# Small sums in two groups, the dt products ahead of turn 4, and the last norm's weights rest on VectorE, in a hybrid decoder layer

## The chip, the cores and the metric

The kernel runs on one core of a Trainium2 chip, in float32. A core has TensorE (PE in the profile, its weight loads PEld), VectorE (DVE), ScalarE (ACT) and GpSimd (POOL); all DMAs here are issued from SyncE's queue (SP). The metric is the device time of one execution in microseconds, the median of three runs. The time before is 1727.1 us (1726.97 to 1727.77).

## What is computed

One decoder layer over 16 learned tokens and 1024 input tokens, D = 1024:

```python
xn = rms_norm(h, mix_pre_g)
proj = xn @ w_in                       # z, xbc, dt, q, k, v
y_ssd = ssd_mixer(z, xbc, dt_raw, ...)           # conv, scan in chunks of 128, rms_norm
y_sb = rms_norm(stick_breaking_attention(q, k, v), sb_norm_g)
mix = concatenate([y_ssd, y_sb]) @ w_out
h = h + rms_norm(mix, mix_post_g)
xn = rms_norm(h, ffn_pre_g)
gu = xn @ w_up
g = causal_dwconv(gu[..., :D_FF], ffn_conv_w, ffn_conv_b)
f = (gelu(g) * gu[..., D_FF:]) @ w_down
h = h + rms_norm(f, ffn_post_g)
return h[:, N_META:]
```

with `rms_norm(x, g) = x * rsqrt(mean(x * x) + EPS) * g`. The two norms inside the mixer (of y_ssd and of y_sb) are not applied to the activations: their gains are multiplied into the rows of `w_out`, and their scales per token, r_ssd and r_sb, are applied to the product.

## The kernel before

Products run on TensorE with both operands cut in two: a high part, rounded on ScalarE, and a **rest**, value minus high part, made by a subtraction on VectorE or GpSimd. A product is then high x high, high x rest of x, rest of w x high. Weights come in blocks of 128 columns; a raw block, its high part and its rest each live in a ring of buffers (`wraw` 2, `whi` 3, `wlo` 3).

**The opening** (lines 231 to 339) has an order written out by hand on all engines: each engine runs its instructions in the order of the source. `norms[i]`, i = 0 to 8, is one block of tokens (block 0 the learned ones). For each: `square` (ScalarE, with a sum along the row), `root` (GpSimd: add EPS, then a power), `norm` (VectorE: times the scale and the gain), `turn_x` (TensorE: eight transposes of 128x128 into two PSUM tiles; ScalarE copies the high halves into `xs`, VectorE subtracts the rests). The products of dt over the first 400 columns (`dt_steps`: 16 products, `pj_dt`) need blocks 0 to 3 in full, high parts and rests, and a weight whose two halves (`wh_dt`) are the high part and the rest. B and C are two column blocks of the next projection; `split_hi` and `split_lo` cut their weights, the rest in two halves on GpSimd. In iteration i of the loop, norm i + 2, turn i and square i + 3 come in this order, with exceptions for i = 3.

**The small sums.** `token_rstd` makes r_ssd and r_sb: `sq` holds squares summed over the blocks of 128 channels, and nine products with a column of ones sum them over the partitions, one column of a PSUM tile each (the program splits each float32 product into two passes). Two VectorE instructions and a power on GpSimd follow. It is called once in the attention (head pair 0, block 2; only TensorE's order is by hand there) and once while the first half of W_out is multiplied, when n is 2 in the loop over `first`, whose steps are 12 products each. `issue_after` puts its products behind the last one issued. Its PSUM tile comes from the ring `mm` that the projections use.

**The last norm of the second sub-layer's input** (lines 1457 to 1600) stands in the last part that is ordered by hand on all engines. `after(t, ...)` is a generator with five steps: square and root of the mixed rows; scale and residual on VectorE; a second square; its root; the second norm. `turn_x2(t, ...)` transposes the result. For t = 8 its steps are run between the first products of the next matrix: `g0_first` (a product into a bank, an evacuation by ScalarE, a second product added into the same bank, an evacuation). `g0` and `u0` are the first blocks of the gate and up weights; `split_1` and `split_2` cut them, high parts on ScalarE and rests on GpSimd. The order of the weights of W_out is not touched.

Of the kernel before, what the change touches and what calls it, by code (L numbers as in the profile page):

```python
# [53 lines left out]
def tile_layer(ctx: ExitStack, tc: tile.TileContext, x, meta, rows, parts,  # L54
# [162 lines left out]
    def dt_steps(hl):  # L217
        for c0, n in CH:
            acc = psum_mm(f"pj_dt_{c0}")
            for k in range(KB):  # L220
                for j in range(2):
                    mm(acc[:32, :n], hl[:, k, :], xs[c0][:, j, k, :n],
                       start=(k == 0 and j == 0), stop=(k == KB - 1 and j == 1))
            nc.vector.tensor_copy(dtT[:, c0:c0 + n], acc[:32, :n])
            yield

    ET = mybir.EngineType
    with tc.tile_pool(name="pre", bufs=3, side="right") as pre, \
# [82 lines left out]
        norm(0)  # L311
        norm(1)
        for i in range(NT + 1):
            if i != 3:
                norm(i + 2)
            turn_x(i)
            square(i + 3)
            root(i + 3)
            if i == 3:
                norm(5)  # L320
            if i == 1:
                hl = wp.tile([P, KB, 32], F32R, tag="whi", name="wh_dt", bufs=WB)
                nc.scalar.activation(hl[:, :, 0:16], raw_dt, AF.Copy)
                nc.gpsimd.tensor_tensor(hl[:, :, 16:32], raw_dt, hl[:, :, 0:16].bitcast(F32), op=ALU.subtract)
                dt_chain = dt_steps(hl)
            if i in (2, 5):
                split_hi("B0" if i == 2 else "C0")
            if i in (2, 3, 5, 6):
                split_lo("B0" if i < 4 else "C0", int(i in (3, 6)))
            if i == 3:  # L330
                chains.append(conv_chain(8, "B0", ws["B0"], True))
            if i == 4:
                run(dt_chain, 1)
            if i in (5, 6):
                run(chains[0][1], 1)
            if i == 6:
                chains.append(conv_chain(10, "C0", ws["C0"], True))
            if i in (7, 8):
                run(chains[1][1], 1)
# [98 lines left out]
        post = []  # L438
        return qkv_steps(p, post), post

    def token_rstd(r, pool, nm):
        pt = psum_mm(f"pt{nm}")
        for t in range(NT + 1):
            a, nr = (M0, 2) if t == 0 else (NM + (t - 1) * P, P)
            mm(pt[:nr, t:t + 1], sq[:, a:a + nr], ones[:, 0:1], start=True, stop=True)
        ms = pool.tile([P, NT + 1], F32, tag="tms", name=f"tms{nm}")
        nc.vector.memset(ms[:, 0:1], 1.0)
        nc.vector.tensor_scalar(ms[:2, 0:1], pt[:2, 0:1], 1.0 / D, EPS, op0=ALU.mult, op1=ALU.add)
        nc.vector.tensor_scalar(ms[:, 1:], pt[:, 1:NT + 1], 1.0 / D, EPS, op0=ALU.mult, op1=ALU.add)
        nc.gpsimd.tensor_tensor(r, ms, nhalf[:, :NT + 1], op=ALU.pow)  # L450
# [553 lines left out]
    for p in range(8):  # L1004
        for i in range(NT):
# [52 lines left out]
            if p == 7 and 2 < i < 6:  # L1058
                run(meta_steps, 1)
            if p == 0 and i == 2:  # L1060
                token_rstd(r_ssd, ap, "a")
    while turn or mix:
        if mix:
            block_mix(*mix.pop(0))
# [33 lines left out]
    ys = [split_y(op, 1, 1, ("yh", "yl", 2))]  # L1098
    y0g = y0s[0]
    nc.vector.tensor_tensor(y0g, y0b, sb_g.unsqueeze(2).to_broadcast([P, 8, 2]), op=ALU.mult)  # L1100
    acc = psum_fa("halo1")[:, 0, 0:256]
    summed = []

    def halo_raw():
# [5 lines left out]
    for n, i in enumerate(first):  # L1110
# [1 line left out]
        if i == 1:  # L1112
            run(second, 2)
        with tc.issue_after(recent[0].ins):
            if n == 2:
                token_rstd(r_sb, est, "b")
            while n > 5 and len(summed) < rows_in:
                halo_raw()
    run(second)
# [346 lines left out]
    for t in range(1, NT + 1):  # L1466
# [44 lines left out]
        elif t == NT:  # L1511
            g0_pair = pair_w("2g0")
            u0.split_1()
            g0.split_2(g0_pair)
            load_raw(1, 1, wp, "wraw", 2)
        run(steps)
        if t == 6:
# [46 lines left out]
        return g0.first_half(ws, psum_fa(f"g0{ws[0]}"), ghalf[jj], part_g)  # L1564

    ga_ = g0_first(0, ("a11", "a12"))
    run(ga_, 1)
    run(norm, 2)
    split_b22(nc.vector)
    turn7 = turn_x2(7, P, xn7, x2_tiles(7))  # L1570
    run(turn7, 1)
# [339 lines left out]
```

## Time and profile before

| | before |
|---|---|
| median of 3 runs | 1727.1 us |
| profiled execution | 1726.21 us, span 1724.3 us |
| TensorE's granted clock, mean | 0.998 |
| VectorE, ScalarE, GpSimd busy | 65%, 48%, 49% |
| HBM read, written | 122.32 MB, 49.73 MB |

The span is the time from the first to the last instruction that was profiled; the profiled execution has its own time, and some 1.9 us lie around its span. In the views, a row has start, length, engine, line, operation, out<-in, and, in brackets, how long the engine stood idle before it and what ended that. Rows of equal instructions are merged (x8). Lengths of neighbours overlap by some hundredths to tenths, since an engine starts an instruction while the one before it drains; the ends of matmuls are modelled. L12 is line 12 of the kernel. `xtp` are the transposes of x, `xn` its norms, `xs` the turned x, `pj_` products of a projection, `x2tp` and `oxn` the transposes and norms of the second sub-layer's input.

### The profile page before, as it was taken

The numbers are of one execution on the slowest core, as the hardware profiler recorded it, in microseconds if no ns is written. First come the engines' busy times: TensorE is split into PE (matmuls) and PEld (weight loads), VectorE is DVE, ScalarE is ACT, GpSimd is POOL, SyncE is SP. The second block draws the span as 40 slices with busy tenths as digits, with TensorE's granted clock in tenths as the row PEclk, the third lists the DMA queues.
The fourth block names the chain that finished last, engine by engine and source line by source line (L and its number), as shares of the span: only waits on it lengthen the run. The fifth ranks groups of instructions, "written<-read, shape, count | busy, mean of one in ns | idle before, by whom it ended". The sixth has DMA issues, their size and how long they took to land. (4 is left out here: it accounts for less than half of the span.)

```text
span 1724.3 us, 28047 instructions
## 1 busy us (share of the span) xinstructions
PE 1703.0 (99%) x11230; PEld 1496.2 (87%) x11230; DVE 1117.8 (65%) x1233; ACT 821.2 (48%) x1370; POOL 850.4 (49%) x642
## 2 busy tenths in 40 slices
PE   7999999999999999999999999999999999999998
PEld 6999889888999998998788788999888888887886
DVE  5752973875676677578530567676666666658777
ACT  5423663555566566557652344433333333344544
POOL 4323664585566575565552122587767777400001
PEclk9999999999999999999999999999999999999999
DMA  4233343231011101112214653233332223395334
GB/s 164 58 111 98 105 127 108 68 105 38 26 38 38 36 28 38 38 50 86 64 68 147 212 174 123 73 107 110 103 92 92 92 92 99 118 330 180 105 113 179
DMA packets 90674, 173.87 MB, mean 101 GB/s; under 512 B 10704, under 2 KB 35816, under 8 KB 90544
## 3 DMA queue, kind: packets, MB, share of 16 engines
q1 hardware_dynamic: 90544, 172.08, 31.4%
q8 instruction: 88, 1.44, 0.4%
q14 instruction: 42, 0.34, 0.1%
HBM read 122.32 MB, written 49.73 MB: 100 GB/s over the span
## 5 line engine op out<-in xcount | busy, mean ns | idle before, releaser
L782 POOL TENSOR_TENSOR bt<-bt,kp 128x256 f32<-128x256 f32 (+7 forms) x128 | 213.0, 1683 | 185.7 <-DVE kp L780 144.3
L780 DVE TENSOR_TENSOR_SCAN kp<-kp,hold 128x272 f32<-128x272 f32 (+7 forms) x128 | 183.5, 1474 | 24.7 <-ACT kp L773 14.3
L1265 POOL TENSOR_TENSOR wlo<-wr,whi 128x1024 fp32r<-128x1024 f32 x43 | 107.7, 2516 | 37.8 <-ACT whi L1264 37.8
L1768 POOL TENSOR_TENSOR fms<-fms 128x1 f32<-128x1 f32 x8 | 2.6, 331 | 223.8 <-ACT dh L1653 197.1
L773 ACT ACTIVATE kp<-z 128x288 f32<-128x288 f32 (+6 forms) x112 | 82.6, 737 | 50.5 <-PE z L772 27.8
L1264 ACT ACTIVATE whi<-wr 128x1024 fp32r<-128x1024 f32 x43 | 45.6, 1060 | 111.5 <-PE fX L1322 67.9
L165 PE MATMUL pj_k<-xs,wh_k 128*128 128x400 f32 (+2 forms) x384 | 95.6, 336 | 0.0
L165 PE MATMUL pj_v<-xs,wh_v 128*128 128x400 f32 (+2 forms) x384 | 95.0, 334 | 0.0
L1394 DVE SCALAR_TENSOR_TENSOR ga<-gr,pp,ga 128x1024 f32<-128x1024 f32 x44 | 71.8, 1632 | 35.1 <-ACT ga L1387 34.3
L165 PE MATMUL pj_q<-xs,wh_q 128*128 128x386 f32 (+2 forms) x384 | 93.8, 331 | 0.0
L796 ACT ACTIVATE th<-tw 128x1024 f32<-128x1024 f32 (+2 forms) x96 | 75.6, 815 | 37.4 <-PE tw L794 37.3
L1653 ACT ACTIVATE dh<-ar 128x512 fp32r<-128x512 f32 x77 | 48.6, 631 | 92.9 <-PE dnB L1731 44.7
L165 PE MATMUL pj_X<-xs,wh_X 128*128 128x400 f32 (+2 forms) x384 | 92.0, 326 | 0.0
L165 PE MATMUL pj_z<-xs,wh_z 128*128 128x386 f32 (+2 forms) x384 | 91.6, 326 | 0.0
L748 DVE CAST qh<-q 128x128 fp32r<-128x128 f32 x64 | 45.5, 712 | 69.9 <-PE z L772 69.6
L1654 DVE TENSOR_TENSOR dl<-ar,dh 128x512 fp32r<-128x512 f32 x77 | 53.2, 691 | 50.2 <-ACT dh L1653 50.2
L966 PE MATMUL mo<-woa,yh 128*128 128x512 f32 x256 | 85.2, 400 | 0.0
L774 ACT ACTIVATE bt<-z 128x288 f32<-128x288 f32 (+6 forms) x112 | 82.9, 740 | 0.0
L794 PE MATMUL tw<-ident,bt 128*128 128x128 f32 x576 | 75.9, 274 | 2.2 <-POOL bt L782 1.6
L809 PE MATMUL av<-th,v 128*64 128x128 f32 x1152 | 77.2, 278 | 0.0
L809 PEld LDWEIGHTS av<-th,v 128*64 128x64 f32 x1152 | 61.5, 136 | 13.8 <-issue 10.9
L794 PEld LDWEIGHTS tw<-ident,bt 128*128 128x128 f32 x576 | 65.5, 141 | 8.6 <-issue 4.0
(560 smaller groups left out, 5623.9 us busy)
## 6 DMA issues: line engine op xcount, KB each, us to landing
wr<-in_w_up SPq DMA_DIRECT2D x44, 512.0 KB
fds<-ga SPq DMA_DIRECT2D x44, 256.0 KB
b<-in_w_down SPq DMA_DIRECT2D x44, 256.0 KB
ar<-fds SPq DMA_DIRECT2D x44, 256.0 KB
fda<-ga SPq DMA_DIRECT2D x33, 256.0 KB
ar<-fda SPq DMA_DIRECT2D x33, 256.0 KB
yk<-yd SPq DMA_DIRECT2D x16, 512.0 KB
wor<-in_w_out SPq DMA_DIRECT2D x12, 512.0 KB
```

The costliest lines, as they stand in the source:

```text
L165: mm(acc[:ncol, :n - s], a[:, k, :ncol], xs[c0][:, b, k, s:n], start=(k == 0 and j == 0), stop=(k == KB - 1 and j == 2))
L773: nc.scalar.activation(kp[:, :, a:a + w], z[:, :, :w], AF.Sigmoid, scale=-QSCALE)
L774: nc.scalar.activation(bt[:, :, a:a + w], z[:, :, :w], AF.Sigmoid, scale=QSCALE)
L780: nc.vector.tensor_tensor_scan(kp[:, j][:, ::-1], kp[:, j][:, ::-1], hold[:, L - n:L][:, ::-1], 0.0, op0=ALU.mult, op1=ALU.max)
L782: nc.gpsimd.tensor_tensor(bt[:, j, 0:m], bt[:, j, 0:m], kp[:, j, 1:m + 1], op=ALU.mult)
L794: nc.tensor.transpose(tw[:, j, b, :], bt[:, j, c0:c0 + P], ident)
L796: nc.scalar.activation(th[:, :, :nb, :], tw[:, :, :nb, :], AF.Copy)
L809: mm(av[halves[j], :], v[:, kb, halves[j]], th[:, j, b, :], start=kb == 0, stop=kb == i)
L966: recent[0] = mm(acc, u[:, k, :], v[:, cs], start=(k == 0 and j == 0), stop=(k == 7 and j == 2))
L1265: nc.gpsimd.tensor_tensor(l, raw, h.bitcast(F32), op=ALU.subtract)
L1394: nc.vector.scalar_tensor_tensor(v, self.g[jj][:, :, i:i + 256], fconv_w[:, j, i:i + 1], v, op0=ALU.mult, op1=ALU.add)
L1654: sub(lo[:, k], raw, hi[:, k].bitcast(F32), op=ALU.subtract)
```

## The change

- Opening: norm 4, square 5 and root 5 move from iterations 2 and 3 to the end of iteration 3, behind turn 3. The cut of B's weights moves from iterations 2 and 3 into iteration 3, with square 6 and root 6 between the two halves of its rest; that of C's from 5 and 6 to 4 and 5. The first 16 dt products go ahead of norm 6 and turn 4 on each engine's order, and take all the high parts of x first, then all the rests.
- `token_rstd` becomes a generator that stops after five of the nine products, and gets its PSUM tile from outside: a tile of the ring `tp` for r_ssd, the unused half of the tile `halo1` for r_sb. It is run in blocks 2 and 3 of head pair 0, and at n = 2 and n = 4.
- The rest of the second raw block of g0 (`g0_pair[1]`, wlo2g) is made by VectorE, in place of GpSimd.
- The first step of the last norm (square and root of t = 8) goes ahead of the first product of g0 and of its evacuation.

```diff
--- before.py
+++ after.py
@@ -217,10 +217,9 @@
     def dt_steps(hl):
         for c0, n in CH:
             acc = psum_mm(f"pj_dt_{c0}")
-            for k in range(KB):
-                for j in range(2):
-                    mm(acc[:32, :n], hl[:, k, :], xs[c0][:, j, k, :n],
-                       start=(k == 0 and j == 0), stop=(k == KB - 1 and j == 1))
+            for i in range(2 * KB):
+                j, k = (i // KB, i % KB) if c0 == 0 else (i % 2, i // 2)
+                mm(acc[:32, :n], hl[:, k, :], xs[c0][:, j, k, :n], start=i == 0, stop=i == 2 * KB - 1)
             nc.vector.tensor_copy(dtT[:, c0:c0 + n], acc[:32, :n])
             yield
 
@@ -311,26 +310,32 @@
         norm(0)
         norm(1)
         for i in range(NT + 1):
-            if i != 3:
+            if i == 4:
+                run(dt_chain, 1)
+            if i not in (2, 3):
                 norm(i + 2)
             turn_x(i)
-            square(i + 3)
-            root(i + 3)
+            if i != 2:
+                square(i + 2 if i == 3 else i + 3)
+                root(i + 2 if i == 3 else i + 3)
             if i == 3:
+                norm(4)
                 norm(5)
             if i == 1:
                 hl = wp.tile([P, KB, 32], F32R, tag="whi", name="wh_dt", bufs=WB)
                 nc.scalar.activation(hl[:, :, 0:16], raw_dt, AF.Copy)
                 nc.gpsimd.tensor_tensor(hl[:, :, 16:32], raw_dt, hl[:, :, 0:16].bitcast(F32), op=ALU.subtract)
                 dt_chain = dt_steps(hl)
-            if i in (2, 5):
-                split_hi("B0" if i == 2 else "C0")
-            if i in (2, 3, 5, 6):
-                split_lo("B0" if i < 4 else "C0", int(i in (3, 6)))
+            if i in (3, 4):
+                split_hi("B0" if i == 3 else "C0")
+            if i in (3, 4, 5):
+                split_lo("B0" if i < 4 else "C0", int(i == 5))
+            if i == 3:
+                square(6)
+                root(6)
+                split_lo("B0", 1)
             if i == 3:
                 chains.append(conv_chain(8, "B0", ws["B0"], True))
-            if i == 4:
-                run(dt_chain, 1)
             if i in (5, 6):
                 run(chains[0][1], 1)
             if i == 6:
@@ -438,9 +443,10 @@
         post = []
         return qkv_steps(p, post), post
 
-    def token_rstd(r, pool, nm):
-        pt = psum_mm(f"pt{nm}")
+    def token_rstd(r, pool, nm, pt):
         for t in range(NT + 1):
+            if t == 5:
+                yield
             a, nr = (M0, 2) if t == 0 else (NM + (t - 1) * P, P)
             mm(pt[:nr, t:t + 1], sq[:, a:a + nr], ones[:, 0:1], start=True, stop=True)
         ms = pool.tile([P, NT + 1], F32, tag="tms", name=f"tms{nm}")
@@ -1058,7 +1064,9 @@
             if p == 7 and 2 < i < 6:
                 run(meta_steps, 1)
             if p == 0 and i == 2:
-                token_rstd(r_ssd, ap, "a")
+                sums = token_rstd(r_ssd, ap, "a", psum_tp("pta")[:, 0, :])
+            if p == 0 and i in (2, 3):
+                run(sums, 1)
     while turn or mix:
         if mix:
             block_mix(*mix.pop(0))
@@ -1098,7 +1106,9 @@
     ys = [split_y(op, 1, 1, ("yh", "yl", 2))]
     y0g = y0s[0]
     nc.vector.tensor_tensor(y0g, y0b, sb_g.unsqueeze(2).to_broadcast([P, 8, 2]), op=ALU.mult)
-    acc = psum_fa("halo1")[:, 0, 0:256]
+    small = psum_fa("halo1")
+    acc = small[:, 0, 0:256]
+    sums = token_rstd(r_sb, est, "b", small[:, 1, :])
     summed = []
 
     def halo_raw():
@@ -1112,8 +1122,8 @@
         if i == 1:
             run(second, 2)
         with tc.issue_after(recent[0].ins):
-            if n == 2:
-                token_rstd(r_sb, est, "b")
+            if n in (2, 4):
+                run(sums, 1)
             while n > 5 and len(summed) < rows_in:
                 halo_raw()
     run(second)
@@ -1511,7 +1521,9 @@
         elif t == NT:
             g0_pair = pair_w("2g0")
             u0.split_1()
-            g0.split_2(g0_pair)
+            nc.scalar.activation(g0_pair[0], raws[0, 1], AF.Copy)
+            nc.vector.tensor_tensor(g0_pair[1], raws[0, 1], g0_pair[0].bitcast(F32), op=ALU.subtract)
+            g0.w["a21"], g0.w["a22"] = [tuple(w[:, s] for w in g0_pair) for s in (LO4, HI4)]
             load_raw(1, 1, wp, "wraw", 2)
         run(steps)
         if t == 6:
@@ -1564,8 +1576,9 @@
         return g0.first_half(ws, psum_fa(f"g0{ws[0]}"), ghalf[jj], part_g)
 
     ga_ = g0_first(0, ("a11", "a12"))
+    run(norm, 1)
     run(ga_, 1)
-    run(norm, 2)
+    run(norm, 1)
     split_b22(nc.vector)
     turn7 = turn_x2(7, P, xn7, x2_tiles(7))
     run(turn7, 1)
```

## The prediction

> **What bounds the kernel now.** I read the page first, then who TensorE waited for, then the timelines of the three places that the diff touches. The page's head says how much is left to win:
>
> ```profile
> span 1724.3 us, 28047 instructions
> PE 1703.0 (99%) x11230; PEld 1496.2 (87%) x11230; DVE 1117.8 (65%) x1233; ACT 821.2 (48%) x1370; POOL 850.4 (49%) x642
> ```
>
> TensorE is busy 1703.0 of 1724.3 us. No edit removes a matmul of the products, so the change can only move the other 21.3 us, or add to them. The view of waits, for TensorE alone, tells where part of them lies (us in total, times, longest):
>
> ```profile
> PE xtp L285 <- DVE xn L273: 9.5, 4, 8.4
> PE tw L794 <- POOL bt L782: 1.6, 1, 1.6
> ...
> PE x2tp L1181 <- DVE oxn L1175: 1.4, 1, 1.4
> ```
>
> and the timeline has the second of them as
>
> ```profile
> 808.90 1.06 PE L794 MATMUL tw<-ident,bt 128*128 128x128 f32 x8 [1.65 <-POOL bt L782]
> ```
>
> The longest, 8.4 us, is the wait for the first norm of x, which the diff leaves alone. Within its reach are the rest of the first row (1.1 us, four turns of x) and the 1.4 us before the last turn of the second sub-layer's input. The 1.6 us in the attention stands where the diff has nothing. So a gain of more than some 4 us isn't there to be had; a loss has no such cap. The rest is three small sums.
>
> **The opening.** The timelines of the first 24 us, TensorE, VectorE, ScalarE, GpSimd (start, us, what):
>
> ```profile
> 9.60 1.97 PE L285 MATMUL xtp<-ident,xn 128*128 128x128 f32 x8 [0.17 <-DVE xn L273]
> ...
> 13.90 1.75 PE L285 MATMUL xtp<-ident,xn 128*128 128x128 f32 x8
> ...
> 16.29 1.09 PE L285 MATMUL xtp<-ident,xn 128*128 128x128 f32 x8 [0.65 <-DVE xn L273]
> ...
> 18.09 2.93 PE L222 MATMUL pj_dt<-xs,wh_dt 128*32 128x400 f32 x15 [0.52 <-DVE xs L292]
> 20.86 1.04 PE L285 MATMUL xtp<-ident,xn 128*128 128x128 f32 x8
> 21.65 0.61 PE L165 MATMUL pj_B<-xs,wh_B 128*128 128x400 f32 x2
> ```
>
> ```profile
> 10.51 1.28 DVE L273 SCALAR_TENSOR_TENSOR xn<-xt,rs_pre,gpre 128x1024 f32<-128x1024 f32 x1 [0.96 <-POOL rs_pre L192]
> ...
> 14.96 1.28 DVE L273 SCALAR_TENSOR_TENSOR xn<-xt,rs_pre,gpre 128x1024 f32<-128x1024 f32 x1
> 16.15 2.48 DVE L292 TENSOR_TENSOR xs<-xtp,xs 128x512 fp32r<-128x512 f32 x4
> ...
> 20.29 2.30 DVE L273 SCALAR_TENSOR_TENSOR xn<-xt,rs_pre,gpre 128x1024 f32<-128x1024 f32 x1 [0.47 <-POOL rs_pre L192]
> ```
>
> ```profile
> 14.35 1.05 ACT L263 ACTIVATE junk<-xt 128x1024 f32<-128x1024 f32 x1
> ...
> 16.34 1.07 ACT L290 ACTIVATE xs<-xtp 128x512 fp32r<-128x512 f32 x2
> ```
>
> ```profile
> 10.88 0.99 POOL L191 TENSOR_SCALAR ms_pre<-ss 128x1 f32<-128x1 f32 x1 [0.41 <-ACT junk L263]
> 11.96 0.57 POOL L192 TENSOR_TENSOR rs_pre<-ms_pre,nhalf 128x1 f32<-128x1 f32 x1
> ...
> 18.53 0.22 POOL L191 TENSOR_SCALAR ms_pre<-ss 128x1 f32<-128x1 f32 x1 [0.32 <-ACT junk L263]
> ...
> 20.23 1.28 POOL L304 TENSOR_TENSOR wl_B<-wr_B,wh_B 128x512 fp32r<-128x512 f32 x1
> ```
>
> What the reader is to see: before, turn 4 (16.29) and the dt products (18.09) each stand for something of VectorE's, and the first product of B starts at 21.65. And VectorE and GpSimd block each other: a GpSimd instruction that takes 0.22 us at 18.53 took 0.99 from 10.88, and ended only after norm 2 did (10.51 + 1.28 = 11.79); norm 6, asked for 0.06 us after the rest of B's weights had started on GpSimd (20.23), took 2.30 us, and ended 1.08 after that rest (21.51).
>
> Now the new order, with these durations. Norm 4 no longer stands ahead of the rests of turns 2 and 3, so those four start at 14.96 and end at 14.96 + 2.48 = 17.44; their high halves are there in time, since ScalarE takes turn 3's as soon as the transposes allow (13.90 + 1.75 = 15.65, then 0.6 for the second half, 16.3). The dt products go first over the high halves, so TensorE can begin at 15.7 and 16 of them, 0.19 us each (2.93 for 15), end near 18.7, against 21.0. That is the 0.5 us of the dt wait gone. Norm 4 runs from 17.4 to 18.65, and turn 4 follows at 18.7 with no wait: so far 16 matmuls and a turn that used to end at 21.0 end at 19.7.
>
> Then it turns. Square 5 now stands behind the high halves of turn 3 on ScalarE: 16.2 to 17.4 with the read of its sum. Its sum reaches GpSimd just after norm 4 has started, so by the row at 10.88 it ends with norm 4, at 18.7, and the power (0.57, after 0.1) at 19.4. So norm 5 can't be asked for before 19.4. Directly behind that power in GpSimd's queue stands the first half of the rest of B's weights (its high part is ScalarE's next 1.05 us after square 5, ready at 18.4). As at 20.23 it starts 0.03 us before the power's end, ahead of the norm: 19.4 to 20.65, and norm 5 ends 1.08 later, at 21.75. Turn 5 starts at 21.8, not 20.86; the product of B 0.79 later, at 22.6, not 21.65: **0.95 us late**. Norm 6 repeats it: its sum waits for norm 5, its scale is there at 22.6, the second half of B's rest takes 22.6 to 23.9, the norm ends near 25.0; TensorE asks for turn 6 after 12 products, at 24.8. I add 0.2 there, and 0.2 for norms 7 and 8 together, which meet C's two halves in the same way. Sum of the opening: **+1.3 us**.
>
> The bounds: if no instruction of GpSimd and VectorE blocked another, the scale of norm 5 would be there before norm 4 ends, norm 5 would follow at 18.6 and turn 5 at 19.9, 0.9 us early. If only the half rest lost the race, norm 5 would run 19.4 to 20.7, and turn 5 start 0.1 early. I take +1.3, as both rows show the blocking, and keep -0.9. The norm, the square and the split that are moved issue no DMA; the load of X's first weights, which takes the buffer of B's, starts when B's rest is done, 23.9 in place of 21.5. The products of B, C and dt, all ahead of X's, hide it; without them X would be 2.4 us late.
>
> The Trainium skill, SBUF — State Buffer, section "SBUF: two separate sides", states the same as a rule: GpSimd and a VectorE operation with two SBUF inputs share one port pair, held for the whole instruction, and the other fully blocks. By that rule the sum above is +1.3; by the order of the engines' work alone it would be -0.9. The trace agrees, with 0.99 us for a 0.22 us instruction.
>
> **The last norm of the second sub-layer.** TensorE, ScalarE, VectorE and GpSimd around 1060 us:
>
> ```profile
> 1061.70 0.39 PE L1336 MATMUL g0a<-b21h,whi 128*128 128x258 f32 x1
> ...
> 1071.90 1.06 PE L1181 MATMUL x2tp<-ident,oxn 128*128 128x128 f32 x8 [1.42 <-DVE oxn L1175]
> ```
>
> ```profile
> 1059.30 1.05 ACT L1264 ACTIVATE whi2g<-wr 128x1024 fp32r<-128x1024 f32 x1
> 1061.04 0.60 ACT L1342 ACTIVATE gr<-g0a 128x516 f32<-128x516 f32 x1 [0.69 <-ACT whi2g L1264]
> 1061.54 1.05 ACT L1162 ACTIVATE t4l<-mb 128x1024 fp32r<-128x1024 f32 x1
> ```
>
> ```profile
> 1060.79 1.63 DVE L1208 TENSOR_TENSOR xc<-xc,xd 128x512 f32<-128x512 f32 x1
> 1065.66 1.28 DVE L1165 SCALAR_TENSOR_TENSOR mb<-mb,rs_mo,gpost 128x1024 f32<-128x1024 f32 x1 [3.25 <-POOL rs_mo L192]
> ...
> 1068.12 1.22 DVE L1230 TENSOR_TENSOR b22l<-b22s,b22h 128x1024 fp32r<-128x1024 f32 x1
> ...
> 1070.47 1.28 DVE L1175 SCALAR_TENSOR_TENSOR oxn<-mb,rs_ff,gffn 128x1024 f32<-128x1024 f32 x1 [0.44 <-POOL rs_ff L192]
> ```
>
> ```profile
> 1059.48 2.39 POOL L1265 TENSOR_TENSOR wlo<-wr,whi 128x1024 fp32r<-128x1024 f32 x1 [1.90 <-ACT whi L1264]
> ...
> 1061.83 2.84 POOL L1265 TENSOR_TENSOR wlo2g<-wr,whi2g 128x1024 fp32r<-128x1024 f32 x1
> 1064.76 0.22 POOL L191 TENSOR_SCALAR ms_mo<-oss 128x1 f32<-128x1 f32 x1
> 1065.06 0.57 POOL L192 TENSOR_TENSOR rs_mo<-ms_mo,nhalf 128x1 f32<-128x1 f32 x1
> ```
>
> The chain to the last turn is square (61.54), its scale (65.06, held up by wlo2g on GpSimd until 64.67), two steps on VectorE, a second square and scale, the norm (70.47), the turn at 71.90. The change gives wlo2g to VectorE, where a subtraction of this size takes 1.22 us (the row at 1068.12), and puts the square ahead of the evacuation of g0a. The square then starts at 1060.3, with whi2g done (1059.30 + 1.05), and its sum is read by 1061.4. GpSimd is free at 1061.87, but xc has waited for it and takes until 1062.4; the sum is done at 1062.65, wlo2g on VectorE takes until 1063.85, the power until 1064.4 (it ends no later if it goes ahead of wlo2g, since the first step on VectorE stands behind both). That step starts at 1064.4 instead of 1065.66, and all behind it is 1.25 us earlier, the norm too: it ends at 70.5, the turn can start at 70.65. TensorE pays a little for the swap: the evacuation of g0a, behind the square, ends at 61.9 and not 61.64, and the second product group, which adds into the same bank, starts 0.25 after 1061.70. So TensorE arrives at the turn at about 70.6 (71.90 - 1.42 + 0.25 = 70.73 by the modelled ends) and finds it ready: **-1.25 us**. The third product group reads wlo2g near 64.9, and has it 1 us earlier. Bounds: -1.6 (the whole wait and the pipeline's own end of the matmul before it), and +0.25 if the chain isn't shortened.
>
> **The small sums.**
>
> ```profile
> 413.69 0.38 PE L794 MATMUL tw<-ident,bt 128*128 128x128 f32 x2
> 414.00 2.07 PE L445 MATMUL pta<-ones,sq 128*2 128x1 f32 x18
> 415.99 0.39 PE L772 MATMUL z<-kh,qh 64*128 64x264 f32 x2
> ```
>
> ```profile
> 939.08 2.07 PE L445 MATMUL ptb<-ones,sq 128*2 128x1 f32 x18
> ...
> 970.33 0.75 DVE L1478 SCALAR_TENSOR_TENSOR mb<-mo,r_sb,mb 128x512 f32<-128x512 f32 x1 [8.68 <-PE mo L966]
> ```
>
> 18 passes at 0.11 us stay 18 passes; split in two groups they pay one more way in and out each, about 0.15 us by the gaps around the first (last transpose to 414.00, last sum to 415.99). Two more groups: **+0.3 us**, between 0 and +0.4. The second half of r_sb's sums comes two steps of 12 products later, 12 us if each took 0.5; r_sb's first reader is at 970.33, 31 us after the first sum. r_ssd is read only by the first half of W_out, head pairs later. What queues behind on VectorE (the reads of the sums) is nothing that TensorE waited for in either place. The new PSUM places are free there: no turn of v falls between the two calls.
>
> **The sum:** +1.3 - 1.25 + 0.3 = +0.35 us on the profiled execution's 1726.21 us (1724.3 of span, 1.9 around it), so 1726.55 for it. That execution lies 0.9 under the median of the runs, 1727.1, which becomes 1727.45.
>
> **Rivals.**
> 1. The opening gains, or at least doesn't lose: norm 5 gets ahead of B's half rest. Then -0.9 to -0.1 in place of +1.3, and the whole is 1725.25 to 1726.05. For it: the race at 19.4 is decided by under 0.1 us. Against it: the row at 20.23 shows who wins when a power stands just ahead. Chance 0.2.
> 2. The last norm doesn't gain: GpSimd's tiny instructions, squeezed between VectorE's, end no earlier, and TensorE still pays 0.25. 1727.1 + 1.3 + 0.25 + 0.3 = 1728.95. For it: the new VectorE work stands on the same chain. Against it: 1.6 us less of subtraction on that chain. Chance 0.13.
> 3. The slower side: TensorE's own pace falls back. Turn 1's transposes took 1.97 us and turn 4's 1.09, so the array began at half pace, for the 5.6 us from 9.60 to about 15.2. My forecast opens a hole of 2.1 us ahead of turn 5 (19.7 to 21.8), where before there was at most 0.65. If that hole is long enough to bring the half pace back for as long again, it costs half of 5.6, 2.8 us: 1730.25. It decides once the hole reaches what the pace needs to fall. Against it: behind the 1.65 us hole eight transposes took 1.06, the full pace. Chance 0.08.
> 4. ScalarE, VectorE and GpSimd have no order by hand in the attention. The sums' new place may shift their order and so the 1.65 us hole there: gone, 1725.8; two or three times over, 1729.1 to 1730.75. Chance 0.12, most of it on the bad side.
>
> On rival 3 the Trainium skill, TensorE: Matmul & The Clock Gate, Part 1, says that the half rate returns only after an idle window of about 3.4 us, so a hole of 2.1 us would not do it. No run so far shows such a fall.
>
> **How the numbers follow.** My forecast has 0.47: 1727.45. Eight in ten lie between 1724.9, a little under rival 1's better end, and 1730.2, rival 3's time. A measurement can tell 0.2%, 3.5 us, from no change. Faster by more needs nearly all holes closed at once: 0.05. Slower by more is the far end of rival 4, or rival 3 or 4 with rival 2: 0.15. The rest, 0.8, is within.
>
> **What would show it.** In the profile after: dt products ending near 18.7; norm 5 taking over 2 us right behind a half rest of B; a wait of about 2 us before turn 5; the product of B at 22.6. At 1070 the wait for oxn down from 1.42 to under 0.3, the VectorE step at 1.25 less than before against its neighbours. Two pieces of pta, 10 and 8 passes. Wrong are my reasons if turn 5 starts before 20.86, if transposes behind the hole take 1.9 us for eight, or if the attention's holes differ by over 1 us.

## The result, and the profile after

| | before | after |
|---|---|---|
| median of 22 runs each | 1726.96 us (1725.35 to 1730.14) | 1724.31 us (1722.3 to 1728.09) |
| ratio, 95% interval | | 0.9988 [0.9982, 0.9993] |
| profiled execution | 1726.21 us, span 1724.3 us | 1723.64 us, span 1721.9 us |

By the ratio the change gains 2.1 us (1.2 to 3.1). That is less than the 0.2%, 3.5 us, of the prediction, but its interval is clear of 1. The median is 0.6 us under the lower end of the predicted range. The page's head and the waits of TensorE after the change (who waited for whom: us in total, times, longest):

```profile
span 1721.9 us, 28048 instructions
PE 1702.0 (99%) x11230; PEld 1495.4 (87%) x11230; DVE 1124.8 (65%) x1234; ACT 821.2 (48%) x1370; POOL 847.1 (49%) x641
```

```profile
PE xtp L284 <- DVE xn L272: 10.4, 4, 8.6
PE halo L1118 <- DMA wor<-in_w_out: 0.6, 1, 0.6
PE tw L800 <- ACT bt L780: 0.5, 1, 0.5
PE tw L800 <- issue: 0.5, 1, 0.5
```

Of the waits of before, the 1.4 us before the last turn is gone, as predicted, and so is the 0.5 us of the dt products. The 1.6 us in the attention, where the diff has nothing, has shrunk to 0.5 ("issue": the profile shows nothing that TensorE waited for). The opening's row has grown by 0.9. The 0.6 us for a DMA of W_out was not in the profile before.

But the waits are not the whole difference. I followed the same instruction of TensorE through both profiles and took its start after minus its start before:

| place in the program | offset, us |
|---|---|
| first transpose | +0.17 |
| first product of B | +1.21 |
| behind the sums for r_ssd (near 422) | +0.83 |
| first transposes behind the hole near 809 | -0.35 |
| products of z behind that, from the third on, near 812 | -1.83 |
| behind the sums for r_sb (near 945) | -1.79 |
| second group of g0a | -0.74 |
| last turn | -2.30 |

So the opening lost 1.04 (0.4 of it was made up by 422), the hole near 809 gave 1.2, the 3.5 us **behind** the hole gave another 1.5, with the same wait of 0.53 us in both, a wait for a DMA near 956 cost 0.63, and the last norm gave 1.3 net of what it cost. Here is the opening after (timeline of TensorE, VectorE, GpSimd):

```profile
16.01 3.79 PE L222 MATMUL pj_dt<-xs,wh_dt 128*32 128x400 f32 x16
19.64 1.04 PE L284 MATMUL xtp<-ident,xn 128*128 128x128 f32 x8
22.04 1.06 PE L284 MATMUL xtp<-ident,xn 128*128 128x128 f32 x8 [1.36 <-DVE xn L272]
22.86 0.61 PE L165 MATMUL pj_B<-xs,wh_B 128*128 128x400 f32 x2
```

```profile
17.57 1.27 DVE L272 SCALAR_TENSOR_TENSOR xn<-xt,rs_pre,gpre 128x1024 f32<-128x1024 f32 x1
19.61 2.28 DVE L272 SCALAR_TENSOR_TENSOR xn<-xt,rs_pre,gpre 128x1024 f32<-128x1024 f32 x1 [0.77 <-POOL rs_pre L192]
```

```profile
17.84 1.08 POOL L191 TENSOR_SCALAR ms_pre<-ss 128x1 f32<-128x1 f32 x1 [2.63 <-ACT junk L262]
19.01 0.57 POOL L192 TENSOR_TENSOR rs_pre<-ms_pre,nhalf 128x1 f32<-128x1 f32 x1
19.54 1.27 POOL L303 TENSOR_TENSOR wl_B<-wr_B,wh_B 128x512 fp32r<-128x512 f32 x1
```

The reader is to see the predicted blocking, instruction by instruction: the sum of square 5 takes 1.08 us on GpSimd beside norm 4, and ends 0.08 after it (17.84 + 1.08 against 17.57 + 1.27). The half rest of B starts 0.07 before norm 5, and norm 5 takes 2.28 in place of 1.28. Turn 5 stands for it.

Near 1060 us (TensorE, VectorE, GpSimd):

```profile
1069.60 1.04 PE L1191 MATMUL x2tp<-ident,oxn 128*128 128x128 f32 x8
```

```profile
1059.80 1.64 DVE L1218 TENSOR_TENSOR xc<-xc,xd 128x512 f32<-128x512 f32 x1
1061.36 1.21 DVE L1525 TENSOR_TENSOR wlo2g<-wr,whi2g 128x1024 fp32r<-128x1024 f32 x1
1063.03 1.28 DVE L1175 SCALAR_TENSOR_TENSOR mb<-mb,rs_mo,gpost 128x1024 f32<-128x1024 f32 x1 [0.46 <-POOL rs_mo L192]
```

```profile
1060.97 0.55 POOL L191 TENSOR_SCALAR ms_mo<-oss 128x1 f32<-128x1 f32 x1
1061.60 1.40 POOL L192 TENSOR_TENSOR rs_mo<-ms_mo,nhalf 128x1 f32<-128x1 f32 x1
```

The power is squeezed behind wlo2g (1.40 us in place of 0.57), and the whole wait before the turn is still gone.

What happened behind the hole is seen in the view that gives TensorE's busy time and its granted clock by stretches (stretch, its length, PE busy, instructions, granted clock, DMA share, GB/s). A granted clock of 1.00 is the full pace, 0.50 half of it. Before:

```profile
807.18:810.59 3.41, 1.23 (x10) 1.00 0.62 167
810.59:814.00 3.41, 3.41 (x16) 0.50 0.38 141
814.00:817.41 3.41, 3.41 (x42) 1.00 0.00 0
```

After:

```profile
805.23:808.65 3.42, 2.94 (x32) 1.00 0.00 0
808.65:812.06 3.41, 2.88 (x24) 1.00 0.81 202
812.06:815.47 3.41, 3.41 (x41) 1.00 0.26 106
```

In the kernel before, the clock is 0.50 for exactly 3.41 us behind the hole: the twelve products of k that start at 810.79 took 2.8 us, and 1.6 after. The page's 40 slices of 43 us each round this away.

### The profile page after: what moved, and what is told of

It reads as the page before. It is cut to its first block, busy times and chain, and to the rows that moved or that the text cites. A ratio compares the mean times of both kernels' runs of the same rounds, so it can differ in the third digit from the quotient of the medians.

```text
span 1721.9 us, 28048 instructions
## 1 busy us (share of the span) xinstructions
PE 1702.0 (99%) x11230; PEld 1495.4 (87%) x11230; DVE 1124.8 (65%) x1234; ACT 821.2 (48%) x1370; POOL 847.1 (49%) x641
## 4 chain that ended last, share of the span: by engine, by line
PE 50%; POOL 0%; DMA 0%; issue 0%; ACT 0%; DVE 0%; DVEq 0%; POOLq 0%; ACTq 0%
PE mo L972 10%; PE fX L1332 10%; PE dnA L1744 7%; PE fY L1332 6%; PE fA L1332 6%; PE dnB L1744 5%; PE g0a L1346 1%; PE av L815 1%; PE tw L800 0%; PE z L778 0%; PE x2tp L1191 0%; POOL wlo L1275 0%; PE g0c L1346 0%; PE g0d L1346 0%; PE u0b L1346 0%; PE u0a L1346 0%
## 5 line engine op out<-in xcount | busy, mean ns | idle before, releaser
L1274 ACT ACTIVATE whi<-wr 128x1024 fp32r<-128x1024 f32 x43 | 45.6, 1060 | 111.4 <-PE fX L1332 67.9
```

## The theories, and the parts alone

After the result I held that the opening and the last norm had done what was predicted (+1.05 and -1.3), and that the small sums and the hole near 809 held the surprise. The rivals: the sums gain by some effect on TensorE's pace, or they are neutral and all of the rest is the hole. Each part alone, with the unchanged kernel beside them:

> The kernel before, unchanged, for a second profile of it and for the width of a comparison with itself. Theory A (the hole in the attention that is 1.65 us before and 0.47 us after is a late load of W_out, and so chance): the wait of TensorE for the turn near 808.9 comes out anywhere from 0.4 to 1.7 us, and the products behind it may run at full pace this time. Theory B (the hole belongs to the kernel before, and the small sums' new place closes it): 1.65 us again, within 0.1, with the half pace of the 12 products behind it. Ratio 1.000 in both.

> Only the opening's part of the change (norm 4, square 5, the cuts of B and C, the dt products). Theory A and B: +1.0 to +1.2 us, as the offset between the two profiles has it behind the opening: turn 5 waits 1.3 to 1.4 us behind norm 5, which takes 2.3 us behind the half rest of B. Rival (the order of the work alone counts, or a luckier pace of the array): 0.5 to 0.9 us faster. Median 1728.0 by the first, 1726.2 by the rival.

> Only the last norm's part (wlo2g by VectorE, the square ahead of the evacuation of g0a). Theory A and B: the 1.42 us wait before the last turn goes, 0.25 us come in front of the second product group: -1.3 us, median 1725.7. Rival (the chain isn't shortened): 0.0 to +0.3 us.

> Only the small sums in two groups, in their new places in PSUM. Theory A: 0 to +0.3 us in the median; the hole in the attention varies as in the kernel before, 0.4 to 1.7 us. Theory B: the hole is below 0.6 us and the products behind it run at full pace, -1.2 to -2.7 us, median 1724.3 to 1725.8.

The edits are the hunks of the change: the opening's (dt_steps and the loop), the last norm's (two hunks), and the sums' (token_rstd and its two callers).

| kernel | median, us (before: 1727.72) | ratio [95%] | us by the ratio |
|---|---|---|---|
| same_as_before | 1727.33 | 1.0002 [0.9993, 1.001] | +0.3 |
| opening_alone | 1728.06 | 1.0003 [0.9992, 1.0013] | +0.5 |
| last_norm_alone | 1726.41 | 0.9995 [0.9986, 1.0003] | -0.9 |
| sums_alone | 1726.18 | 0.999 [0.9982, 0.9999] | -1.7 |

The parts add to -2.1, the whole measured -2.1. Only the sums are clear of 1 by themselves, just so, and on the side opposite to the predicted +0.3. The profile of the unchanged kernel shows how one group of sums can cost something (stretches as above; its group of 18 passes runs from 941.30 to 943.23):

```profile
939.94:943.35 3.41, 3.41 (x26) 1.00 1.02 414
943.35:946.76 3.41, 3.41 (x10) 0.50 0.88 334
946.76:950.17 3.41, 3.41 (x16) 1.00 0.23 80
```

And the profile of the kernel before, whose group runs from 939.08 to 941.01, over an edge between two stretches:

```profile
936.88:940.30 3.42, 3.42 (x23) 1.00 0.97 373
940.30:943.71 3.41, 3.41 (x20) 1.00 1.02 364
```

TensorE counts as busy all the time, and waits for nothing. Yet in the first execution eight products start in the stretch at 0.50, 0.427 us apart, where those of the next stretch are 0.227 apart: about 1.6 us lost. (The counts in the view also hold instructions that only reach into a stretch.)

## Is it the length of the group, or its place?

The sums done twice over (both results are the same), in one go at each place, and in four groups (the changed token_rstd with three stops, run in blocks 2 to 5 and at n = 2 to 5); the third run, later, has the single groups in the new places in PSUM:

```diff
-        for t in range(NT + 1):
+        for t in 2 * list(range(NT + 1)):
```

> The kernel before, with each group of small sums done twice in one go: 36 passes over one column, 4 us, in each of the two places. Theory C (such passes do not keep the array's pace up: a long enough stretch of them lets it fall to half for some 3 us): half pace right behind both groups in the profile, 1.2 to 1.8 us each, and 4.0 us for the passes themselves; the kernel before has it in some executions already, so +5.5 to +7 us in the median. Rival (the sums cost their passes only): +4.0 us, full pace behind both.

> The same doubled sums in four groups of 10, 8, 10 and 8 passes in each place, products between them, in the PSUM places of the change. Theory C: full pace behind all eight groups, +4.0 us for the passes, +0.4 for the ways in and out, less the falls that the kernel before has in some executions (0 to 1.7): +2.5 to +4.5 us, 2 to 3 us faster than in one group. Rival (only the passes count): +4.4 us, as in one group.

> The small sums twice in one go, 36 passes, but in the PSUM places of the change (ring tp, the free half of halo1). It tells the split from the place. Theory C (the unbroken stretch of one-column passes lets the pace fall): half pace behind or in both groups, as in the old place, +5 to +9 us in the median. Rival (the old place in the ring of the projections held TensorE up): full pace, near the four groups, +2 to +4.5 us.

| kernel | ratio [95%] | us | granted clock of 0.5 behind the sums, in the profile |
|---|---|---|---|
| one group of 36 | 1.005 [1.0031, 1.0068] | +8.6 | 6.83 us at both places |
| one group of 36, new places | 1.0053 [1.004, 1.0067] | +9.2 | 3.41 us at the first place, 6.83 at the second |
| four groups of 10, 8, 10, 8 | 1.0017 [1.0008, 1.0026] | +2.9 | none |

The same passes cost three times as much in one piece. The split does it; the place in PSUM makes no difference that these runs can tell. The clock's own records in the trace show more: in all 17 profiles each change of the clock stands on a grid of 3.413 us (the first stretch of full clock in the profile before is 233 steps long, 795.305 us), and the grid lies anew in every execution. So the theory became: at each edge of the grid, TensorE gets 0.5 for the next stretch if ordinary passes filled less than about half of the last one; passes of one column count as nothing. The rival: an unbroken stretch of some 1.9 us of small passes is what does it. The next kernel tells them apart, with short groups and little between them, and two others try the theory on a group that no edit had touched, the 16 passes of four columns in the attention of the learned tokens (`avm`, near 875 us):

```diff
+        for n, t in enumerate((3 if nm == "a" else 1) * list(range(NT + 1))):
+            if nm == "a" and n in (4, 9, 13, 18, 22):
+                for k in range(2):
+                    mm(pt[:, 112:512], xs[0][:, 0, k, :P], xs[0][:, 0, k, :400], start=True, stop=True)
```

> The sums near 414 us done three times over, 54 passes in six groups of 8 or 10, with two ordinary products of 400 columns (0.37 us, into a part of the tile that nobody reads) between the groups; those near 940 as before. No group is longer than 1.1 us, but ordinary passes fill only about a third of the whole, some 8 us. The theory of windows: the stretch of the grid behind the first one that is full of this has a granted clock of 0.5, so 0.5 near 418 to 425 for at least 3.4 us, in this one look. The rival, that an unbroken stretch of about 1.9 us is what does it: 1.00 there, as with the four groups that stood 4 to 8 us apart. Time: 7 us more for the work itself, and 1.7 to 3.5 on top by the first.

The timeline of TensorE in it, and the stretches of the grid:

```profile
414.22 0.95 PE L448 MATMUL pta<-ones,sq 128*2 128x1 f32 x8
415.03 0.61 PE L446 MATMUL pta<-xs 128*128 128x400 f32 x2
415.49 1.17 PE L448 MATMUL pta<-ones,sq 128*128 128x1 f32 x10
```

```profile
414.46:417.87 3.41, 3.41 (x28) 1.00 0.19 74
417.87:421.28 3.41, 3.41 (x16) 0.50 0.00 0
421.28:424.70 3.42, 3.42 (x17) 0.50 0.00 0
424.70:428.11 3.41, 3.41 (x23) 0.50 0.00 0
428.11:431.52 3.41, 3.41 (x12) 0.50 0.00 0
431.52:434.93 3.41, 3.37 (x30) 1.00 0.00 0
```

Up to the edge at 417.87 no group is longer than 1.17 us, and from that edge on, the first behind the first full stretch, the clock is at 0.5 for four stretches (in which the groups of ten passes take 2.13 us each). So no unbroken 1.9 us is needed for a fall; the share stands. The theory doesn't say how a stretch that is at 0.5 already counts: the third of the four held 0.64 of ordinary passes, at half pace, and the fourth was at 0.5 again. (Its one time, 1738.74, is 11.7 over the median before; 7 were expected for the work itself. The rest was not taken apart: the clock is in it, and a wait of 1.4 us for a load of W_out near 968.)

```diff
-            for p in range(8):
-                mm(av[:, 4 * p:4 * p + 4], mv[:, p, :], wc[:, 4 * p:4 * p + 4], start=True, stop=True)
+        for h in range(2):
+            if h:
+                yield
+            av = psum_av("avm")
+            for p in range(4 * h, 4 * h + 4):
+                mm(av[:, 4 * p:4 * p + 4], mv[:, p, :], wc[:, 4 * p:4 * p + 4], start=True, stop=True)
```

> The 16 four-column products of the learned tokens' attention (avm, 1.94 us in one group near 875 us) in two groups of eight, on top of the kernel with the old opening and the new order of dt. The theory of windows (the granted clock is set for stretches of 3.41 us on a grid that runs freely; a stretch in which ordinary passes fill less than about half is followed by one at 0.5) says: a group of 1.94 us fills over 1.75 us of one stretch in about 56 of 100 positions and then costs 1.7 us, so 0.95 on the mean; the two groups (about 1.05 each, 0.15 more for a second way in and out) never do: 0.8 us less than the same kernel with one group, 0.9967 of the kernel before, and a granted clock of 1.00 all the way from the opening to the last 10 us. The rival, that only the sums of squares have this effect, says 0.15 more than with one group, 0.9973, and 0.5 in some profiles near 877.

> The kernel with the old opening and the new order of dt once more, beside the one with avm in two groups. Both theories: 0.9972 of the kernel before, as it was, give or take 0.001. The theory of windows: near 877 a granted clock of 0.5 if at least 1.75 us of avm lie in one stretch of the grid, and 1.00 if not, to be read from the grid's edges in this profile; the same holds for no other place, since its sums stand in groups of 1.03 and 0.81 us.

The second of them (timeline, and stretches):

```profile
872.10 1.94 PE L867 MATMUL avm<-wcm,meta_v 16*128 16x4 f32 x16
```

```profile
870.90:874.31 3.41, 3.41 (x26) 1.00 0.00 0
874.31:877.72 3.41, 3.41 (x26) 0.50 0.34 90
877.72:881.14 3.42, 3.42 (x21) 1.00 0.21 71
```

avm lay wholly in one stretch, and the next had 0.5. With avm in two groups the clock was 1.00 from the opening to the last 2 us. The times don't tell the two apart: 1722.82 us, 0.998 [0.9972, 0.9989], with two groups, 1723.48 us, 0.998 [0.9971, 0.9989], with one. The expected 0.8 us is less than these intervals, so the gain of that split in time is open. That it avoids falls is seen beyond the one profile: the granted clock of every execution is on record as a mean over the span, and over eleven executions each it is 0.9995 with two groups and 0.9982 with one.

Over the 17 profiles, leaving out stretches that were at 0.5 already and the last 7 us, I worked out for every stretch the share of ordinary passes and transposes (from one pass's start to the next, small passes and waits as nothing):

| share of the stretch | stretches | followed by 0.5 |
|---|---|---|
| up to 0.47 | 20 | 20 |
| 0.48 to 0.51 | 5 | 3 |
| over 0.51 | all others | 0 |

A group of 18 (1.93 us) that lay wholly in one stretch was followed by 0.5 each time, three of three; parted by an edge, 1.79 at most in one stretch, never in ten. Of the groups of 10 and 8 (1.04 and 0.82) none of 36 was. A group that fills 1.8 of 3.41 us or more of a stretch does it: by its length a group of 1.93 has some 1.7 us of 3.41 to start in for that, every second execution. Two places, half of the time, 1.7 us each: an estimate of 1.7 us is the mean gain of the split, where -1.7 was measured (-0.2 to -3.1). (Only three of the thirteen groups of 18 in these profiles lay wholly in one stretch.) The two more ways in and out cost next to nothing: near 940 the sums put off the products behind them by 2.11 us in one piece and by 2.13 in two, and near 414 the split is 0.1 cheaper.

The mean clock of every execution bears this out. At 0.001 of clock for 1.7 us of lost pace, an estimate that holds where TensorE sets the time, the 35 executions of the kernel before beside sums_alone (0.9971) and the 11 of sums_alone (0.9983) differ by 2.0 us (0.9 to 3.2). Over all 88 executions of the kernel before that stand beside the experiments it is 0.9972, over the 22 of the changed kernel 0.9984: 2.1 us (1.3 to 2.9), as much as the whole change gained. With the opening alone it is 0.9972, with the last norm alone 0.9977.

The Trainium skill, TensorE: Matmul & The Clock Gate, Part 1, describes such a gate, with windows of 3413 ns that run freely and the half rate after an idle window. The grid agrees (3.413 us). That the window must be idle doesn't: a stretch with 1.5 us of full products in it was followed by the half rate (939.94 to 943.35 above).

## Why the hole near 809 closed

One reading of the opening's +0.5 beside its local +1.05 was that the hole near 809 depends on where TensorE's program stands. The trace records DMA packets of kind "instruction", 16 KB each, 88 of them beside the 22,460 instructions of PE and PEld. I took them for fetches of TensorE's own code; the next run, which adds 64 instructions to TensorE alone and so moves one of them by 4.4 us, bears that out. One such fetch falls near the load of a block of W_out (`wor`, 512 KB) that ScalarE's `woa` reads, ahead of the evacuations that the attention needs. ScalarE's waits in the kernel before, 796 to 812 us:

```profile
ACT woa L894 <- DMA wor<-in_w_out: 1.1, 1, 1.1
```

After, there is no such line. To move only the fetch, I put 32 small products into an unread tile ahead of the first square, where TensorE waits for x anyway:

```diff
+        spare = psum_mm("spare")
+        for _ in range(32):
+            mm(spare[:32, :NM], identb[:NM, :32], identb[:NM, :NM], start=True, stop=True)
```

> The kernel before, with 32 products of 16 columns into an unread tile while TensorE waits for the first norm: 64 instructions, no time of their own. Theory D (the hole in the attention is made by a fetch of TensorE's own code, 16 KB that stand before the last packets of a load of W_out on one DMA engine): all later fetches come 64 instructions earlier in the work, about 5 us there, ahead of that load, so it lands within 3.4 us as in the kernels with the new opening, ScalarE does not wait for it, the hole before the turn is 0.6 us or less, the products behind it run at full pace, -1 to -2.7 us at this place. Theory A (chance): 1.4 to 1.7 us or anything else. Theory B (the order of the engines' work): 1.65 us again.

The hole in its timeline of TensorE:

```profile
809.17 1.06 PE L797 MATMUL tw<-ident,bt 128*128 128x128 f32 x8 [0.47 <-issue]
```

0.47 us, not 1.65, with nothing else changed. Its time is 1.0006 [0.9997, 1.0015] all the same: in the profiled execution all three groups of small passes were followed by 0.5 (at 416.35, 877.15 and 942.01). So the hole depends on where the code stands in the program; a gain in time by this edit isn't shown, and its interval leaves no room for one of 1.2 us. Its mean clock is 0.9966, beside 0.9973 for the kernel before, a difference at the edge of chance. From the records of single packets (start of the fetch and last packet of the load, from the load's issue), ten of the profiles:

| profile | fetch, us | load landed, us | hole, us |
|---|---|---|---|
| before | +2.47 | +4.29 | 1.65 |
| same_as_before | +2.36 | +4.11 | 1.48 |
| sums_alone | +2.42 | +4.17 | 1.50 |
| last_norm_alone | +1.16 | +4.90 | 2.26 |
| order_only_last_norm | +2.33 | +4.07 | 1.43 |
| code_shifted | -1.93 | +3.22 | 0.47 |
| opening_alone | +2.87 | +3.24 | 0.52 |
| after | +3.05 | +3.23 | 0.47 |
| old_opening_new_dt_order | +3.13 | +3.18 | 0.62 |
| old_opening_again | +2.58 | +3.14 | 0.4 |

A fetch that starts 1.2 to 2.5 us behind the load's issue goes with a landing about 1 us later; one ahead of it, or 2.6 us and more behind, doesn't. The other seven profiles fall in with it: with the fetch at +3.0 to +3.1 the load landed at +3.1 to +3.4 (best_rest_only_last_norm, avm_in_two_groups, half_rest_behind_root_6), at +1.1 to +1.9 it landed at +4.4 to +5.0 (the three with sums done twice), and at -4.6 at +3.2 (sums_thrice_with_products_between). The border is thin: +2.47 is late and +2.58 isn't. How the late load reaches the turn, and how the new order of the dt products moves the fetch by half a microsecond against the load, was not traced.

## The opening and the last norm, taken apart

```diff
-            if i in (3, 4, 5):
-                split_lo("B0" if i < 4 else "C0", int(i == 5))
+            if i in (4, 5):
+                split_lo("C0", int(i == 5))
             if i == 3:
                 square(6)
                 root(6)
+                split_lo("B0", 0)
                 split_lo("B0", 1)
```

> The changed kernel, the first half of the rest of B's weights behind root 6 on GpSimd in place of behind root 5. Theory E (norm 5 takes 2.28 us because that half rest holds what VectorE needs): norm 5 takes 1.3 us, turn 5 starts about 1.1 us earlier after its scale's power (1.3 to 1.4 us after that power's end instead of 2.5); the third product of B then waits about 1 us for the half rest, so the opening as a whole gains 0.5 us at most. Rival (norm 5 is slow for another cause): 2.2 us and more again.

VectorE and TensorE in it:

```profile
20.27 1.28 DVE L272 SCALAR_TENSOR_TENSOR xn<-xt,rs_pre,gpre 128x1024 f32<-128x1024 f32 x1 [0.76 <-POOL rs_pre L192]
...
22.32 2.30 DVE L272 SCALAR_TENSOR_TENSOR xn<-xt,rs_pre,gpre 128x1024 f32<-128x1024 f32 x1 [0.30 <-POOL rs_pre L192]
```

```profile
21.70 1.06 PE L284 MATMUL xtp<-ident,xn 128*128 128x128 f32 x8 [0.98 <-DVE xn L272]
...
23.59 0.45 PE L165 MATMUL pj_B<-xs,wl_B 128*128 128x400 f32 x1 [0.46 <-POOL wl_B L303]
```

With the half rest out of the way, norm 5 takes 1.28 us again: the half rest was what held it, shown. But little comes of it: turn 5 still waits 0.98 us, in place of 1.36, norm 6 meets the rests and takes 2.30, as in the changed kernel (2.31), and the third product of B now waits 0.46 for its rest. The one time, 1725.79, is too coarse for half a microsecond.

Of the last norm's two edits, the order alone (square ahead of the evacuation, rest still on GpSimd), and the reverse, on top of the version below:

> The kernel before with the first step of the last norm ahead of the evacuation of g0a, the weights' rest still on GpSimd. Expected by the sum in the prediction: the square runs 1.2 us earlier, but its sum still waits on GpSimd behind wlo2g, so the step on VectorE comes no earlier; the wait before the last turn stays within 0.3 us of 1.42, less the 0.25 us that now come before the second product group. Rival (the order made the gain): the wait falls below 0.5 us.

> The kernel with the old opening and the new dt order, sums in two groups, wlo2g on VectorE, but the last norm's square behind the evacuation of g0a as before. Expected: the 0.1 to 0.25 us before the second product group go; the square ends at about the same 1.2 us later than in the change, but GpSimd's and VectorE's work in front of the step on VectorE ends only 0.1 to 0.2 us later, so the wait before the last turn is 0 to 0.3 us. Time -3.5 to -5 us against before, within 0.3 us of the kernel with the new order.

```diff
+    run(norm, 1)
     run(ga_, 1)
-    run(norm, 2)
+    run(norm, 1)
```

The last turn with the order alone:

```profile
1071.75 1.06 PE L1181 MATMUL x2tp<-ident,oxn 128*128 128x128 f32 x8 [1.16 <-DVE oxn L1175]
```

1.42 became 1.16 only because TensorE lost 0.25 ahead of it. With VectorE's rest alone the turn stands for less than 0.2 us and no gap opens before the second group of g0a: 1722.76 us, 0.9973 [0.9961, 0.9985], level with the version below, which has both edits (0.9972). VectorE's rest does all of the work.

## A version with the old opening

If the opening loses 1.05 and the new order of dt closes the hole, keep the one without the other: the sums and the last norm as after, the opening as before, the dt products with the high parts first.

> The changed kernel with the opening of before, but the first dt products over the high parts first, then the rests. By the two openings' rows: the dt products begin at 17.14 as before, do the high parts while VectorE makes the rests of turn 3, and end near 20.1 instead of 21.0; norm 5 ends at 19.82; so turn 5 and the product of B come 0.7 us earlier than before and 1.8 earlier than in the changed kernel. With the last norm's -1.3 and the sums' part: -3 to -4 us against before, -0.8 to -1.8 against the changed kernel, if the fetch of code in the attention falls well; with the 1.65 us hole back, about level with the changed kernel.

| kernel | median, us | ratio [95%] |
|---|---|---|
| old_opening_new_dt_order | 1722.59 (before 1727.5) | 0.9972 [0.9961, 0.9984] |
| the same, once more | 1723.48 (before 1727.0) | 0.998 [0.9971, 0.9989] |
| after | 1724.31 (before 1726.96) | 0.9988 [0.9982, 0.9993] |

It is 3.5 to 4.8 us under before. That it also beats the changed kernel is likely and not shown: the two were not timed side by side, and their intervals touch. Its first product of B starts at 20.80, against 21.65 before and 22.86 after: the dt wait is gone and norm 5 isn't late.

## Why the prediction was wrong, by its own steps

**The opening** (+1.3) was right in kind and nearly in size: +1.04 to the first product of B. Norm 5 at 2.28 us right behind a half rest, turn 5 behind 22.0, the product of B at 22.86 (22.6 named). The dt products ended at 19.6, not 18.7, mostly by the clock: it rose in this execution at 17.64, in that of before at 15.28, so the first 1.6 us of these products ran at half pace. Rival 1 is out.

**The last norm** (-1.25) was right: -1.3 by the difference of offsets with its +0.25 counted in, and the wait gone whole. The stall of the second group was +0.25, as named. The reason for the order was wrong: that edit gains nothing.

**The small sums** (+0.3) is the step that failed. "18 passes at 0.11 us stay 18 passes" prices the passes and not what they do to the clock of those behind them: the 1.7 us on the mean that the split avoids was not in the sum. The 0.3 for two more ways in and out was not there either. Behind it stands the premise that the change "can only move the other 21.3 us": the 1703.0 us in which TensorE counts as busy hold passes at half pace, and can shrink.

**"The 1.6 us in the attention stands where the diff has nothing"** failed too: in the profiled pair 1.2 us of it went, with a load of W_out that landed a microsecond sooner where a code fetch had moved, and with it 1.5 us behind the hole. Of the rivals, the fourth ("gone, 1725.8") comes nearest in place and sign, but not by the cause that it named, the sums' new place: with the sums alone the hole was still 1.50 us.

**Rival 3** had the right mechanism in the wrong place, and the argument against it misread the trace. "Behind the 1.65 us hole eight transposes took 1.06, the full pace": they did, because the clock changes only at the next edge, at 810.59, 0.6 us behind their end; the products from there on ran at half the clock. The fall was in the profile of the kernel before, where the prediction says that no run so far shows one; in the profiled pair, taking the hole away gained what rival 3 feared to lose. Ahead of turn 5, where it was feared, the hole of 1.36 us was too short, and an edge at 21.05 parts it. The sentence of the Trainium skill (TensorE: Matmul & The Clock Gate, Part 1) that the half rate comes back after an idle window was taken as a bound; it is none here.

With the sum's own terms as the traces have them it reads +1.05 - 1.3, and - 1.7 for the sums on the mean: -1.95, or -3.15 with the 1.2 of the hole, where the runs give -2.1 (-1.2 to -3.1). What the closed hole is worth on the mean stays open: with the code shifted it closed and gained nothing, and with the opening alone it closed too and +0.5 was measured (-1.4 to +2.2). The half clock behind the hole comes in some executions only. What the 0.63 us for a DMA of W_out near 956 is stays open too; of the other profiles only sums_thrice_with_products_between has it, with 1.4 us.

## What to carry to other kernels

On a kernel whose TensorE is busy 99% of the time, count the busy time as something that can shrink, and look at the granted clock in stretches of a few microseconds around holes and around groups of tiny matmuls, not only at waits: such a group costs what the passes behind it lose. Keep groups of passes with few columns well under half of 3.4 us, and put ordinary products between them. Where two engines block each other, look which of them wins the start before moving work, and try each half of an edit by itself: two of the four parts here carried the gain, one carried a loss.

## What was not expected of the hardware

- Four-column and one-column passes count as idle time for TensorE's clock, though the profile shows the engine busy: 20 of 20 stretches of 3.413 us with at most 0.47 of ordinary passes were followed by a clock of 0.5.
- Transposes of 128 columns count as work: in code_shifted the clock rose at 13.58, and from 9.6 to there TensorE had done nothing but such transposes.
- The clock's first rise lies between 12.8 and 21.8 us in these executions. Much of the spread of single runs, about 5 us in both kernels, goes with the clock behind it: the kernel before took 1728.9 us on the mean of its 23 executions at 0.996, 1726.5 in 27 at 0.998 and 1724.8 in 11 at 0.999.
- Where a 16 KB fetch of TensorE's own code started 1.1 to 2.5 us behind the issue of a 512 KB load, the load landed 4.1 to 5.0 us after its issue, in place of 3.1 to 3.4.
